# A tuned encoder trunk on one core: the first gated product kept in SBUF, the softmax's row maximum kept in PSUM, and one broadcast issued later

## The chip, the cores and the metric

The kernel runs on one core of a Trainium2 chip. The metric is the device time of one execution in microseconds, and the number compared is the median of several executions. Everything is float32 in memory; matrix products run in fp32r, each as three products of a high and a low part (hi x hi, hi x lo, lo x hi), so that nearly every operand has to be split into two tiles first.

## The reference

One encoder layer is applied to a prompt of 1024 tokens and to a sample of 256 tokens, both of width 1024. Cut to what matters here:

```python
y_a = deltanet_branch(...) @ w_up_a
y_b = spatial_gating_branch(...) @ w_up_b
merged = sigmoid(gate_a) * y_a + sigmoid(gate_b) * y_b
x = x + merged @ w_out
...
s = einsum('blhd,bmhd->bhlm', q, k) * XA_HEAD_DIM ** -0.5   # 4 heads, 256 memory tokens
p = softmax(s, axis=-1)
x = x + einsum('bhlm,bmhd->blhd', p, v).reshape(...) @ w_o
h = rmsnorm(x, norm_ffn_w)
gu = h @ ffn_w_gate_up
x = x + (silu(gu[..., :D_FF]) * gu[..., D_FF:]) @ ffn_w_down
```

A final RMS norm follows.

## The kernel before

**Layout.** Activations lie with channels on partitions, as tiles of 128 channels by tokens. `BLOCKS` cuts the 1280 tokens into two prompt blocks of 512 (b = 0, 1) and the sample's 256 (b = 2). A product of one output tile with one block is a chain of 128x512 or 128x256 matmuls into one PSUM bank. Two pools of four banks each (`pm`, `pq`) serve the whole program.

**What sets the order.** TensorE's instructions run in the order in which the Python code issues them. Main work is a generator; side work (norms, attention, loads) is a second set of generators that is let in when a planned clock, advanced by the cost of each issued matmul, passes the side's due time. Constants such as `LAGS2` are such due times, in planned nanoseconds. The other engines and the queues that issue transfers each work in one order of their own, which a scheduler derives from that code; an instruction that waits holds up all that stand behind it on its engine or queue. SyncE (SP) issues nearly all loads, ScalarE (ACT) some stores.

**Splitting.** `split` makes the high part on ScalarE (L125) and the low part on VectorE (DVE) or GpSimd (POOL) (L126); the low part is a subtraction of two SBUF tensors.

**The two ways up.** Both gates were computed earlier and stored in DRAM as `gtd`. `up_b` computes the spatial-gating branch's 8 x 3 products (24 jobs, tile m and block b). For each it loads the gate with `gate_load` into one of four `stage` slots, multiplies in place (L1132), and stores the result to DRAM (`tbd`, L1133, on ACT's queue). `up_a`, next, does the 24 products of the other branch: `merge_load` fetches its own gate (`ga`, L1200) and the stored result (`gb`, L1201); L1326 multiplies, and L1328 (prompt, into `mt`) or L1330 (sample) adds the two. While `up_b` runs, the side `load_ya` fetches `yod` and `sgd` (L1152), multiplies them (L1157) and splits them into the operands of `up_a`. `mt` has two tiles of the pool `hp`, under the tags hi0 and lo0; the memory's split tokens had these tags until `up_b` begins. Then comes the output projection (`Seven`), which needs `mt` split and combined.

**Attention.** For each of four heads and each 128 tokens, `scores` makes a 128x256 score tile in a bank. VectorE takes the negated row maximum (L1527) into a small SBUF tile `st`, multiplies it with the norm's factor `rstd`, also in SBUF (L1528); ScalarE exponentiates in the bank (L1530); VectorE takes the reciprocal (L1531) and scales into `e` (L1532), which frees the bank.

**Norms.** `Norm.rest` makes the mean on TensorE, the root on VectorE (L225 to L229, result `nst`), waits `lag2` of planned time, then issues the broadcast of the root over 128 partitions as matmuls of `nst` with the identity; VectorE then scales each tile (L285). The third norm, ahead of the feed-forward part, runs for each block as a side; `LAGS2` holds its `lag2` for the three blocks. `ff_first` is the first feed-forward step: its products with the sample come last in it.

Of the kernel before, what the change touches and what calls it, by code (L numbers as in the profile page):

```python
# [8 lines left out]
F32 = mybir.dt.float32  # L9
# [3 lines left out]
ALU = mybir.AluOpType  # L13
AX = mybir.AxisListType
# [3 lines left out]
P = 128  # L18
D = 1024
KT = D // P  # L20
NP, NS = 1024, 256
NTOK = NP + NS
NCH = NTOK // P
NMEM = 256
# [30 lines left out]
class Trunk:  # L55
# [54 lines left out]
    def mm3(self, ps, pairs, start=True, stop=True, more=False):  # L110

        last = len(pairs) - 1
        for i, (wh, wl, xh, xl) in enumerate(pairs):
            self.mm(ps, wh, xh, start and i == 0, False, more)
            self.mm(ps, wh, xl, False, False, more)
            self.mm(ps, wl, xh, False, stop and i == last, more)
            yield 0

    def tr(self, out, x, ident):
        self.clock += 64  # L120
        self.nc.tensor.transpose(out, x, ident)  # L121


    def split(self, hi, lo, src, eng=None):
        self.last_hi = self.nc.scalar.activation(hi, src, AF.Copy).ins  # L125
        (eng or self.nc.vector).tensor_tensor(out=lo, in0=src, in1=f32(hi), op=ALU.subtract)  # L126
# [37 lines left out]
def trunk_kernel(ctx: ExitStack, tc: tile.TileContext, a):  # L164
    nc = tc.nc
    V, S, G, T, SY = nc.vector, nc.scalar, nc.gpsimd, nc.tensor, nc.sync
# [3 lines left out]
    def pool(name, bufs=1, **kw):  # L170
        if kw.get("space") != DRAM:
            kw["reuse_waits"] = "tile"
        return tc.tile_pool(name=name, bufs=bufs, **kw)
# [3 lines left out]
    hp = ctx.enter_context(pool("h"))  # L177
    pm = ctx.enter_context(pool("pm", 4, space=PSUM))
    pq = ctx.enter_context(pool("pq", 4, space=PSUM))
    dp = ctx.enter_context(pool("dram", space=DRAM))  # L180
# [5 lines left out]
    n = 0  # L186
# [31 lines left out]
    def bank(p=pq, tag="b"):  # L218
        return p.tile([P, 512], F32, tag=tag, name="bank")
# [190 lines left out]
    yod = dp.tile([HEADS, P, NTOK], F32, name="yod")  # L410
    sgd = dp.tile([HEADS, P, NTOK], F32, name="sgd")
    gtd = dp.tile([16, P, NTOK], F32, name="gtd")
    tbd = dp.tile([KT, P, NTOK], F32, name="tbd")
    grd = dp.tile([2, 40, P], F32, name="grd")
    sqd = dp.tile([3, HEADS, P, NS], F32, name="sqd")

# [15 lines left out]
    ab = sp.tile([P, NCH, 16], F32, name="ab")  # L432
# [620 lines left out]
    def staging(n):  # L1053
        staged.append(0)
        return stage[:, len(staged) % 4, :n]
# [50 lines left out]
    def half_wk(w, i, k):  # L1106
        return wk(w, 4 * i + k)

    jobs = [(m, b) for m in range(KT) for b in range(3)]
    gates = []  # L1110

    def gate_load():
        if len(gates) < len(jobs):
            m, b = jobs[len(gates)]
            t0, n = BLOCKS[b]
            tb = staging(n)
            SY.dma_start(tb, gtd[8 + m, :, t0 : t0 + n])
            gates.append(tb)

    def up_b():  # L1120
        gate_load()
        for j, (m, b) in enumerate(jobs):
            if b == 0 and m % 2 == 0:
                w = K.take()
            gate_load()
            t0, n = BLOCKS[b]
            hi, lo = yb_h[b]
            ps = bank(pm)[:, :n]
            yield from mm3(ps, [(*half_wk(w, m % 2, k), hi[:, k, :], lo[:, k, :]) for k in range(4)])
            if m % 2 == 0 and b == 1:  # L1130
                K.ahead()
            V.scalar_tensor_tensor(out=gates[j], in0=gates[j], scalar=1.0, in1=ps, op0=ALU.add, op1=ALU.mult)  # L1132
            S.dma_start(tbd[m, :, t0 : t0 + n], gates[j])  # L1133

    y_h = []
    ues = ExitStack()
# [35 lines left out]
    def rest():  # L1172
        for m in range(1, KT):
            yield from mem_k(m)
        for h in range(HEADS):
            yield from mem_v(h)
        yield from up_b()
# [11 lines left out]

    up = K.up  # L1190
    merged = []
    mt = [hp.tile([P, KT, 512], F32, tag=tag, name="mt") for tag in ("hi0", "lo0")]
    smp_h = tuple(hp.tile([P, KT, NS], F32R, tag=tag, name=tag) for tag in ("hi2", "lo2"))

    def merge_load():
        if len(merged) < len(jobs):
            m, b = jobs[len(merged)]
            t0, n = BLOCKS[b]
            ta, tb = (up.tile([P, 512], F32, tag=f"g{x}", name=f"g{x}", bufs=4)[:, :n] for x in "ab")
            SY.dma_start(ta, gtd[m, :, t0 : t0 + n])  # L1200
            SY.dma_start(tb, tbd[m, :, t0 : t0 + n])  # L1201
            merged.append((ta, tb))

    class Seven:
# [306 lines left out]
    def attend(h, qh, ql, kh, kl, vh, vl, o_h):  # L1511
        es = {}

        def scores(b, c):
            g = 0 if b < 2 else 1
            t0 = BLOCKS[b][0]
            ts = slice(t0 + c * P, t0 + (c + 1) * P)
            ps = bank()[:, :NMEM]
            pairs = []
            for j in range(2):  # L1520
                ms = slice(j * 512 + g * NMEM, j * 512 + (g + 1) * NMEM)
                pairs.append((qh[:, j, ts], ql[:, j, ts], kh[:, ms], kl[:, ms]))
            for _ in mm3(ps, pairs):
                pass
            st = tp.tile([P, 4], F32, tag="st", name="st", bufs=8)
            r = rstd[:, t0 // P + c : t0 // P + c + 1]
            V.tensor_reduce(out=st[:, 3:4], in_=ps, axis=AX.X, op=ALU.max, negate=True)  # L1527
            V.tensor_tensor(out=st[:, 0:1], in0=st[:, 3:4], in1=r, op=ALU.mult)  # L1528
            e = tp.tile([P, NMEM], F32, tag="e", name="e", bufs=6)
            S.activation(ps, ps, AF.Exp, scale=r, bias=st[:, 0:1], accum_out=st[:, 1:2])  # L1530
            V.reciprocal(st[:, 2:3], st[:, 1:2])  # L1531
            V.tensor_scalar(out=e, in0=ps, scalar1=st[:, 2:3], scalar2=None, op0=ALU.mult)  # L1532
            es[b, c] = e

        def some(todo):
            if todo:
                b, c = todo.pop(0)
                scores(b, c)
                scores(b, c + 1)
                return A1  # L1540
            return 0

        todo = [(b, c) for b, (_, n) in enumerate(BLOCKS) for c in range(0, n // P, 2)]
        yield some(todo)
        yield some(todo)
        for b, (t0, n) in enumerate(BLOCKS):
            g = 0 if b < 2 else 1
            yield some(todo) + A2
            ppt = [bank(), bank()]
            pth, ptl = (tp.tile([P, 2, 512], F32R, tag=f"pt{i}", name=f"pt{i}") for i in range(2))  # L1550
            for j in range(2):
                for c in range(n // P):
                    tr(ppt[j][:, c * P : (c + 1) * P], es[b, c][:, j * P : (j + 1) * P], ident)
                split(pth[:, j, :n], ptl[:, j, :n], ppt[j][:, :n])
            yield some(todo) + A3
            for j in range(2):
                po = bank()[:, :n]
                pairs = []
                for mt in range(2):
                    vs = slice((2 * g + mt) * 256 + j * P, (2 * g + mt) * 256 + (j + 1) * P)  # L1560
                    pairs.append((vh[:, vs], vl[:, vs], pth[:, mt, :n], ptl[:, mt, :n]))
                for _ in mm3(po, pairs):
                    pass
                if o_h is None:
                    oo = tp.tile([P, 512], F32, tag="oo", name="oo", bufs=2)[:, :n]
                    S.activation(oo, po, AF.Copy)
                    S.dma_start(od[2 * h + j, :, t0 : t0 + n], oo)
                else:
                    hi, lo = o_h[b]
                    split(hi[:, 2 * h + j, :], lo[:, 2 * h + j, :], po)  # L1570
                yield A4
# [50 lines left out]
    op = OutProj(o_h, h3)  # L1622
# [638 lines left out]
MIX = 6500  # L2261
A1, A2, A3, A4 = 1200, 800, 2000, 600
DEC, CONV = 1200, 600
FIRST_W, PACES, LAGS2 = 9000, (600, 1300, 600), (2800, 9500, 7000)
LAGX = (26000, 17000, 9000)
LAG0, LAGF, LAGF2, PACEF = 7500, (8000, 6000, 1500), (9000, 9000, 2800), 1000

# [80 lines left out]
```

## Time and profile before

| | |
|---|---|
| median of 3 runs | 2226.89 us (2223.06 to 2227.9) |
| profiled execution, whole | 2224.42 us |
| its span in the trace | 2222.6 us |
| PE (matmul) busy | 2179.2 us, 98% of the span |
| PEld (weight load) busy | 1906.1 us, 86% |
| DVE, ACT, POOL busy | 1391.3, 866.9, 555.3 us |
| mean granted TensorE clock | 0.997 |

Times in the profile are microseconds from the span's start. A row of the timeline gives start, length, engine, line, operation, output and inputs, shape, and in brackets how long the engine had sat idle and what released it; "x2" merges two instructions. Lengths of successive matmuls overlap, since they are pipelined, so what a product costs TensorE is read from start to start.

### The profile page before, as it was taken

Reading aid. Unit: us, or ns where it says so; the run is one execution under the profiler, and the core shown is the slowest. Engines: PE = TensorE matmul, PEld = TensorE weight load, DVE = VectorE, ACT = ScalarE, POOL = GpSimd, SP = SyncE. Lnnn points to the kernel's source line nnn. Section 1 sums busy time; section 2 is a strip of 40 time slices with the busy share of each in tenths; the row PEclk is TensorE's granted clock in tenths of the full one; section 3 lists DMA queues with packets and bytes.
Section 4 is the critical chain, followed back from the end, with each engine's and each line's share of the span. In section 5 each row is a group of like instructions: output and inputs, shape, how many; then the busy total and the mean of one; then the engine's idle time right before and its main releaser. Section 6 shows DMA issues by size and latency. Waiting matters only on the chain.

```text
span 2222.6 us, 32341 instructions
## 1 busy us (share of the span) xinstructions
PE 2179.2 (98%) x12416; PEld 1906.1 (86%) x12416; DVE 1391.3 (63%) x2657; ACT 866.9 (39%) x1625; POOL 555.3 (25%) x358
## 2 busy tenths in 40 slices
PE   6999999999999999999999999999999999999998
PEld 5988889898988899888888888888888888888888
DVE  7767777786974864687654546734443444378575
ACT  5434153443525443124544423422322232343453
POOL 3010000000000000034421332466666666200031
PEclk9999999999999999999999999999999999999999
DMA  5222332223234455971421441222222222493631
GB/s 181 82 82 74 100 77 89 75 72 97 74 112 127 154 148 167 332 236 39 166 86 57 158 152 57 95 86 82 87 81 76 78 86 90 141 347 127 204 109 58
DMA packets 192821, 263.52 MB, mean 119 GB/s; under 512 B 72394, under 2 KB 102682, under 8 KB 192666
## 3 DMA queue, kind: packets, MB, share of 16 engines
q1 hardware_dynamic: 172826, 232.34, 31.8%
q10 hardware_dynamic: 19840, 29.11, 3.6%
q8 instruction: 97, 1.59, 0.3%
q14 instruction: 58, 0.48, 0.1%
HBM read 183.24 MB, written 78.16 MB: 118 GB/s over the span
## 4 chain that ended last, share of the span: by engine, by line
PE 82%; DVE 6%; issue 5%; DMA 4%; ACT 1%; POOL 1%; SPq 0%; POOLq 0%; ACTq 0%; DVEq 0%
PE bank L108 81%; PE bank L121 1%; DMA tbd<-stage 1%; DMA braw<-gq 1%; DVE wlo L1232 0%; DVE xf L126 0%; DMA stage<-gtd 0%; DVE lo L126 0%; DVE x L1441 0%; DMA t<-sgd 0%; DMA gb<-tbd 0%; DMA r<-in_w_out 0%; DVE nacc L250 0%; DVE wlo L126 0%; DVE nt L285 0%
## 5 line engine op out<-in xcount | busy, mean ns | idle before, releaser
L108 PE MATMUL bank<-hi,whi 128*128 128x512 f32 (+1 forms) x1976 | 701.9, 355 | 0.0
L108 PE MATMUL bank<-hi,wlo 128*128 128x512 f32 (+1 forms) x1976 | 687.0, 348 | 0.0
L108 PE MATMUL bank<-lo,whi 128*128 128x512 f32 (+1 forms) x1976 | 686.8, 348 | 0.0
L108 PEld LDWEIGHTS bank<-hi,wlo 128*128 128x128 f32 x1976 | 373.6, 189 | 48.8
L108 PEld LDWEIGHTS bank<-hi,whi 128*128 128x128 f32 x1976 | 374.4, 189 | 43.8 <-issue 0.2
L108 PEld LDWEIGHTS bank<-lo,whi 128*128 128x128 f32 x1976 | 374.6, 190 | 43.4 <-issue 0.2
L125 ACT ACTIVATE whi<-raw 128x1024 fp32r<-128x1024 f32 (+1 forms) x136 | 137.0, 1010 | 258.3 <-PE bank L108 219.2
L126 POOL TENSOR_TENSOR wlo<-raw,whi 128x1024 fp32r<-128x1024 f32 x65 | 157.2, 2420 | 307.4 <-ACT whi L125 307.4
L108 PE MATMUL bank<-bhl,whi 128*128 128x512 f32 x408 | 125.9, 390 | 0.1
L126 DVE TENSOR_TENSOR wlo<-raw,whi 128x1024 fp32r<-128x1024 f32 (+1 forms) x71 | 81.7, 1151 | 66.0 <-ACT whi L125 65.6
L126 POOL TENSOR_TENSOR wlo<-x,whi 128x1024 fp32r<-128x1024 f32 x40 | 97.4, 2435 | 47.6 <-ACT whi L125 47.6
L2013 DVE TENSOR_TENSOR x<-x,bank 128x512 f32<-128x512 f32 x21 | 14.5, 688 | 125.5 <-ACT x L1808 125.5
L108 PEld LDWEIGHTS bank<-bhl,whi 128*128 128x128 f32 x408 | 76.5, 188 | 16.5 <-ACT whi L125 0.5
L615 DVE SCALAR_TENSOR_TENSOR acc<-craw,sm,acc 128x510 f32<-128x510 f32 (+1 forms) x96 | 72.9, 759 | 25.9 <-ACT acc L613 24.2
L1821 DVE SCALAR_TENSOR_TENSOR t<-t,x 128x512 f32<-128x512 f32 x42 | 64.2, 1530 | 28.4 <-ACT t L1820 28.4
L108 PE MATMUL bank<-bhl,wlo 128*128 128x512 f32 x204 | 79.7, 391 | 0.7 <-DVE wlo L126 0.5
L125 ACT ACTIVATE whi<-x 128x1024 fp32r<-128x1024 f32 (+1 forms) x48 | 49.0, 1025 | 79.9 <-PE bank L108 73.7
L250 DVE TENSOR_TENSOR nacc<-nacc,nsq 128x512 f32<-128x512 f32 (+1 forms) x68 | 58.0, 852 | 34.0 <-ACT nsq L249 32.8
L1830 DVE SCALAR_TENSOR_TENSOR t<-bank,t 128x512 f32<-128x512 f32 (+1 forms) x44 | 24.5, 558 | 82.5 <-PE bank L108 82.5
L108 PE MATMUL bank<-bhl,ahl 128*128 128x512 f32 x312 | 75.0, 395 | 0.0
L883 POOL COPY UT<-U 64x512 f32<-64x512 f32 x20 | 14.9, 752 | 238.8 <-PE bank L108 235.8
L982 ACT ACTIVATE gs<-bank 128x512 f32<-128x512 f32 (+1 forms) x60 | 31.1, 518 | 108.3 <-PE bank L108 102.9
(373 smaller groups left out, 4578.5 us busy)
## 6 DMA issues: line engine op xcount, KB each, us to landing
raw<-in_w_gu SPq DMA_DIRECT2D x44, 512.0 KB, 3.5
braw<-gq SPq DMA_DIRECT2D x14, 1024.0 KB, 7.2
raw<-in_w_g SPq DMA_DIRECT2D x20, 512.0 KB, 3.3
gq<-t SPq DMA_DIRECT2D x33, 256.0 KB, 2.0
gtd<-gs ACTq DMA_DIRECT2D x32, 256.0 KB, 2.2
w<-in_w_dn SPq DMA_DIRECT2D x8, 1024.0 KB, 12.4
raw<-in_w_qkv SPq DMA_DIRECT2D x12, 512.0 KB, 3.6
gq<-r SPq DMA_DIRECT2D x22, 256.0 KB, 2.1
```

The costliest lines, as they stand in the source:

```text
L108: self.nc.tensor.matmul(out, l, r, start=start, stop=stop, skip_group_check=more)
L121: self.nc.tensor.transpose(out, x, ident)
L125: self.last_hi = self.nc.scalar.activation(hi, src, AF.Copy).ins
L126: (eng or self.nc.vector).tensor_tensor(out=lo, in0=src, in1=f32(hi), op=ALU.subtract)
L250: (eng or V).tensor_tensor(out=self.acc, in0=self.acc, in1=sq, op=ALU.add)
L615: V.scalar_tensor_tensor(out=dst, in0=src, scalar=wj, in1=dst, op0=ALU.mult, op1=ALU.add)
L883: G.tensor_copy(Um[q, hs, :], U[d][q, hs, :])
L982: S.activation(t, ps, AF.Tanh, scale=0.5)
L1821: V.scalar_tensor_tensor(out=t, in0=t, scalar=1.0, in1=src, op0=ALU.add, op1=ALU.mult)
L1830: V.scalar_tensor_tensor(out=out, in0=u, scalar=sign, in1=t, op0=ALU.mult, op1=ALU.mult)
L2013: V.tensor_tensor(out=c22, in0=c22, in1=pe, op=ALU.add)
```

## The change

Three independent edits.

1. The gated result of `up_b` for the two prompt blocks is written straight into `mt` (allocated earlier for that), not to `stage` and DRAM, and `up_a` adds to it in place. Only the sample's result still goes through `tbd`. `up_b` also loads its gates two jobs ahead where it loaded one ahead.
2. The negated row maximum goes into column 256 of the bank that holds the scores, not into `st`.
3. `LAGS2` of the sample is 9500 where it was 7000, so the broadcast of its root is issued later.

```diff
     def up_b():
-        gate_load()
+        mt.extend(hp.tile([P, KT, 512], F32, tag=tag, name="mt") for tag in ("hi0", "lo0"))
+        for _ in range(2):
+            gate_load()
...
-            V.scalar_tensor_tensor(out=gates[j], in0=gates[j], scalar=1.0, in1=ps, op0=ALU.add, op1=ALU.mult)
-            S.dma_start(tbd[m, :, t0 : t0 + n], gates[j])
+            out = mt[b][:, m, :] if b < 2 else gates[j]
+            V.scalar_tensor_tensor(out=out, in0=gates[j], scalar=1.0, in1=ps, op0=ALU.add, op1=ALU.mult)
+            if b == 2:
+                S.dma_start(tbd[m], out)
...
-            ta, tb = (up.tile([P, 512], F32, tag=f"g{x}", name=f"g{x}", bufs=4)[:, :n] for x in "ab")
+            ta = up.tile([P, 512], F32, tag="ga", name="ga", bufs=4)[:, :n]
             SY.dma_start(ta, gtd[m, :, t0 : t0 + n])
-            SY.dma_start(tb, tbd[m, :, t0 : t0 + n])
+            if b < 2:
+                tb = mt[b][:, m, :]
+            else:
+                tb = up.tile([P, NS], F32, tag="gb", name="gb", bufs=3)
+                SY.dma_start(tb, tbd[m])
...
-            ps = bank()[:, :NMEM]
+            pb = bank()
+            ps, mx = pb[:, :NMEM], pb[:, NMEM : NMEM + 1]
...
-            V.tensor_reduce(out=st[:, 3:4], in_=ps, axis=AX.X, op=ALU.max, negate=True)
-            V.tensor_tensor(out=st[:, 0:1], in0=st[:, 3:4], in1=r, op=ALU.mult)
+            V.tensor_reduce(out=mx, in_=ps, axis=AX.X, op=ALU.max, negate=True)
+            V.tensor_tensor(out=st[:, 0:1], in0=mx, in1=r, op=ALU.mult)
...
-FIRST_W, PACES, LAGS2 = 9000, (600, 1300, 600), (2800, 9500, 7000)
+FIRST_W, PACES, LAGS2 = 9000, (600, 1300, 600), (2800, 9500, 9500)
```

Lines behind the edits move by up to ten: L1152 becomes L1158, L1200 becomes L1205, L1201 becomes L1210, L1218 becomes L1227.

On TensorE the only instruction that moves is the broadcast of edit 3. Before it stood one step ahead of the end of the product with `b21`, the second half of the first block's operand (hi_12890 here):

```order
L108 MATMUL bank<-hi_12890,wlo 128x512
L108 MATMUL bank<-cst,nst 128x128 x2
L108 MATMUL bank<-hi_12890,whi 128x512
L108 MATMUL bank<-lo_12891,whi 128x512
L108 MATMUL bank<-hi_12890,wlo 128x512
L108 MATMUL bank<-hi_12892,whi 128x512
```

Now that product (hi_12842 here) is finished first, and nine matmuls with the second block's `b22` (hi_12844) stand ahead of the broadcast too:

```order
L108 MATMUL bank<-hi_12842,wlo 128x512
L108 MATMUL bank<-hi_12844,whi 128x512
L108 MATMUL bank<-lo_12845,whi 128x512
L108 MATMUL bank<-hi_12844,wlo 128x512
L108 MATMUL bank<-hi_12844,whi 128x512
L108 MATMUL bank<-lo_12845,whi 128x512
L108 MATMUL bank<-hi_12844,wlo 128x512
L108 MATMUL bank<-hi_12844,whi 128x512
L108 MATMUL bank<-lo_12845,whi 128x512
L108 MATMUL bank<-hi_12844,wlo 128x512
L108 MATMUL bank<-cst,nst 128x128 x2
L108 MATMUL bank<-hi_12844,whi 128x512
```

The broadcast is issued twelve matmuls of 128x512 later. What VectorE does with it moves too. Before, from the end of the root (`nst`) on, where x_12580 is the sample's tile and x_12578 and x_12579 are those of the prompt blocks:

```order
L229 SCALAR_TENSOR_TENSOR nst<-bank,nst 128x2
L126 TENSOR_TENSOR lo_12893<-x_12578,hi_12892 128x1024
L285 SCALAR_TENSOR_TENSOR x_12580<-x_12580,sm,bank 128x256 x2
L1830 SCALAR_TENSOR_TENSOR t<-bank,t 128x512
L126 TENSOR_TENSOR lo_12895<-x_12580,hi_12894 128x256
L285 SCALAR_TENSOR_TENSOR x_12580<-x_12580,sm,bank 128x256 x4
```

Now, from the same place, the sample's tile being x_12532:

```order
L229 SCALAR_TENSOR_TENSOR nst<-bank,nst 128x2
L1840 SCALAR_TENSOR_TENSOR t<-bank,t 128x512
L126 TENSOR_TENSOR lo_12845<-x_12530,hi_12844 128x1024
L285 SCALAR_TENSOR_TENSOR x_12532<-x_12532,sm,bank 128x256 x4
L126 TENSOR_TENSOR lo_12847<-x_12532,hi_12846 128x256
L285 SCALAR_TENSOR_TENSOR x_12532<-x_12532,sm,bank 128x256
L126 TENSOR_TENSOR lo_12847<-x_12532,hi_12846 128x256
L285 SCALAR_TENSOR_TENSOR x_12532<-x_12532,sm,bank 128x256
L126 TENSOR_TENSOR lo_12845<-x_12530,hi_12844 128x1024
L126 TENSOR_TENSOR lo_12847<-x_12532,hi_12846 128x256
L1831 SCALAR_TENSOR_TENSOR t<-t,bank 128x512
L285 SCALAR_TENSOR_TENSOR x_12532<-x_12532,sm,bank 128x256 x2
```

Other work of the prompt blocks goes ahead of the sample's scalings, and the last two of the eight come behind a 128x512 step of the gate. On SP's queue, in `up_b`, the fetches of `load_ya` stood in pairs behind each other:

```order
L1152 DMA t_8951<-yod 128x2x512
L1152 DMA t_8952<-sgd 128x2x512
L1152 DMA t_8987<-yod 128x2x512
L1152 DMA t_8988<-sgd 128x2x512
L1117 DMA stage<-gtd 128x512 x2
L1117 DMA stage<-gtd 128x256
```

Now each pair stands behind one more load of a gate:

```order
L1158 DMA t_8950<-yod 128x2x512
L1158 DMA t_8951<-sgd 128x2x512
L1117 DMA stage<-gtd 128x512
L1158 DMA t_8985<-yod 128x2x512
L1158 DMA t_8986<-sgd 128x2x512
L1117 DMA stage<-gtd 128x512
L1117 DMA stage<-gtd 128x256
```

The second pair now waits behind a gate's load, which needs a free `stage` slot. Of `up_a`'s loads in this queue the sixteen `gb` loads of the prompt are gone.

More of the change, by code (lines that the diff above doesn't have):

```diff
@@ L412, in trunk_kernel @@
     gtd = dp.tile([16, P, NTOK], F32, name="gtd")
-    tbd = dp.tile([KT, P, NTOK], F32, name="tbd")
+    tbd = dp.tile([KT, P, NS], F32, name="tbd")
     grd = dp.tile([2, 40, P], F32, name="grd")
@@ L1118, in gate_load @@
             gates.append(tb)
+    mt = []
     def up_b():
-        gate_load()
+        mt.extend(hp.tile([P, KT, 512], F32, tag=tag, name="mt") for tag in ("hi0", "lo0"))
+        for _ in range(2):
+            gate_load()
         for j, (m, b) in enumerate(jobs):
@@ L1191, in trunk_kernel @@
     merged = []
-    mt = [hp.tile([P, KT, 512], F32, tag=tag, name="mt") for tag in ("hi0", "lo0")]
     smp_h = tuple(hp.tile([P, KT, NS], F32R, tag=tag, name=tag) for tag in ("hi2", "lo2"))
```

## The prediction

> **What bounds the kernel now.** First the page's busy times, then what TensorE waited for, then the stretches around the three edits.
>
> ```profile
> PE 2179.2 (98%) x12416; PEld 1906.1 (86%) x12416; DVE 1391.3 (63%) x2657; ACT 866.9 (39%) x1625; POOL 555.3 (25%) x358
> PE bank L108 <- DVE nst L229: 7.2, 5, 2.3
> PE bank L108 <- DVE e L1532: 2.0, 2, 1.8
> PE bank L108 <- DVE stage L1132: 1.7, 4, 0.8
> PE bank L108 <- DVE ga L1326: 1.0, 2, 0.5
> ```
>
> TensorE is the bound: of the 2222.6 us span 2222.6 - 2179.2 = 43.4 us are idle, so no edit that leaves its products alone can win more than its own small part of that. The four waiting rows (total, times, longest) name the places: a root (nst), the softmax (e), and the two ways up (stage, ga). The edits touch one wait of the first row and the other three rows. The change is thus worth single microseconds; 0.2% of this kernel, about what a measurement can tell from no change, is 4.45 us.
>
> **Edit 1, the ways up.** The windows give length, then PE, PEld and DVE busy, and near the end clock, DMA share and GB/s:
>
> ```profile
> 880.00:900.00 20.00, 20.00 (x107) 17.24 (x106) 12.51 (x14) 4.24 (x4) 0.00 (x0) 1.00 0.98 321
> 900.00:920.00 20.00, 18.75 (x97) 15.22 (x96) 10.62 (x15) 3.38 (x4) 0.00 (x0) 1.00 0.85 288
> 920.00:940.00 20.00, 19.57 (x97) 16.18 (x96) 11.44 (x16) 3.49 (x4) 2.40 (x1) 1.00 1.04 381
> 940.00:960.00 20.00, 19.04 (x100) 15.84 (x99) 18.32 (x26) 4.53 (x7) 2.40 (x1) 1.00 0.81 270
> SPq L1117 <- DMA tbd<-stage: 35.1, 10, 6.7
> DVE stage L1132 <- DMA stage<-gtd: 9.3, 5, 3.3
> DVE t L1157 <- DMA t<-sgd: 5.1, 5, 1.7
> tbd<-stage ACTq DMA_DIRECT2D x16, 256.0 KB, 4.1
> gb<-tbd SPq DMA_DIRECT2D x11, 256.0 KB, 4.4
> ```
>
> The DMA engines are full from 880 to 940. SP stood 35.1 us on gate loads, because a stage slot is free only once its store to tbd has landed; VectorE then stood 9.3 us on late gates, and TensorE ran out of banks. PE idle from 900 to 960 is 1.25 + 0.43 + 0.96 = 2.64 us. From start to start it is more:
>
> ```profile
> 904.10 0.28 PE L108 MATMUL bank<-yb,wlo 128*128 128x256 f32 x1
> 905.16 0.70 PE L108 MATMUL bank<-yb,whi 128*128 128x512 f32 x2 [0.78 <-DVE stage L1132]
> 946.74 0.39 PE L108 MATMUL bank<-yhi,wlo 128*128 128x512 f32 x1
> 947.61 0.39 PE L108 MATMUL bank<-yhi,whi 128*128 128x256 f32 x1 [0.48 <-DVE ga L1326]
> 987.33 1.06 ACT L125 ACTIVATE xf<-mt 128x1024 fp32r<-128x1024 f32 x1 [4.83 <-PE bank L108]
> 988.42 2.41 DVE L126 TENSOR_TENSOR xf<-mt,xf 128x1024 fp32r<-128x1024 f32 x1 [5.67 <-ACT xf L125]
> ```
>
> A 256-wide matmul otherwise starts 0.12 us after the last, a 512-wide one 0.23 us, so the first gap costs 1.06 - 0.12 = 0.94 where 0.78 is listed, the second 0.87 - 0.23 = 0.64 where 0.48 is listed: 0.16 more each. For the six waits that is 2.64 + 6 x 0.16 = 3.6 us. The change takes away 16 stores and 16 loads of 256 KB, 8.4 MB of what the full DMA engines move here; a slot is then freed by L1132 itself, not by a store's landing, and the gates are fetched one job earlier. L1132 writes the same number of elements, and hi0 and lo0 are free, since the products that read the memory's tokens stand earlier on TensorE: that costs nothing. The sample's eight stores and loads stay. I take all 3.6. Bounds: 1.7, the stage row alone (late t<-sgd may still hold up VectorE), and 4.0, if the slow start after each gap (about 0.07) goes too. Does the gain survive? The last two rows say yes: when up_a ends, ACT and VectorE have idled 4.83 and 5.67 us and are released by TensorE's own last product, so the work behind shifts with it.
>
> **Edit 2, the row maximum.** The first five rows are of the first head's start, the others of the last head's start:
>
> ```profile
> 1112.13 2.41 POOL L126 TENSOR_TENSOR wlo<-raw,whi 128x1024 fp32r<-128x1024 f32 x1
> 1112.20 2.36 DVE L1528 TENSOR_TENSOR st<-st,rstd 128x1 f32<-128x1 f32 x1
> 1115.41 0.39 PE L108 MATMUL bank<-hi,wlo 128*128 128x512 f32 x1
> 1116.02 1.68 PE L108 MATMUL bank<-kv,q 128*128 128x256 f32 x12 [0.22 <-DVE e L1532]
> 1116.92 0.16 DVE L1528 TENSOR_TENSOR st<-st,rstd 128x1 f32<-128x1 f32 x1
> ...
> 1118.00 0.48 DVE L1532 TENSOR_SCALAR e<-bank,st 128x256 f32<-128x256 f32 x1
> ...
> 1246.89 1.25 DVE L1528 TENSOR_TENSOR st<-st,rstd 128x1 f32<-128x1 f32 x1
> 1248.51 0.85 DVE L1528 TENSOR_TENSOR st<-st,rstd 128x1 f32<-128x1 f32 x1
> ...
> 1247.84 0.39 PE L108 MATMUL bank<-hi,wlo 128*128 128x512 f32 x1
> 1250.01 2.00 PE L108 MATMUL bank<-kv,q 128*128 128x256 f32 x12 [1.78 <-DVE e L1532]
> ```
>
> A product of two columns of one element takes 0.16 us, but 2.36 when GpSimd runs a subtraction: it ends with that (1114.56 against 1114.54). Both of L1528's inputs lie in SBUF. The root's L228 shows what one input in PSUM does (length min/median/max in ns):
>
> ```profile
> L228 DVE TENSOR_TENSOR bank<-bank,nst x30: 160/170/171, 11.5 to 2214.7; 128x4 f32<-128x4 f32 x21, 128x2 f32<-128x2 f32 x9
> L228 DVE TENSOR_TENSOR cw<-cw x30: 155/166/169, 219.3 to 868.6; 128x8 f32<-128x8 f32 x30
> L228 DVE TENSOR_TENSOR sums<-sums x9: 148/155/2355, 50.2 to 126.2; 128x4 f32<-128x4 f32 x6, 128x2 f32<-128x2 f32 x3
> ```
>
> With two SBUF inputs 2355 ns occurs, in PSUM never over 171. So L1528 should take 0.16 to 0.17 everywhere. First place: 0.61 - 0.23 = 0.38 us from start to start, gone, since e comes 2.2 us earlier. Last head: 2.17 - 0.23 = 1.94 us lost, and the twelve matmuls then take 0.32 longer than at 1116.02, behind the second bank. An undisturbed chain puts e 1118.00 - 1116.92 = 1.08 us behind L1528, so e runs from 1247.97 to 1248.45, TensorE starts at 1248.51 where it could at 1248.07, and 0.44 stays: 1.94 - 0.44 + 0.32 = 1.8. Together 2.2 us. Bounds: 0.4 (the first place alone, if GpSimd then holds up a neighbour) and 2.7 (no rest). In PSUM the operand costs 170 - 166 = 4 ns or 170 - 155 = 15 ns; the maximum's write into PSUM is not in the trace, and the nearest rows, these, allow 0.02 us a tile, on VectorE's own time.
>
> [...]
>
> **Edit 3, the broadcast.**
>
> ```profile
> 1387.05 0.39 PE L108 MATMUL bank<-hi,wlo 128*128 128x512 f32 x1
> 1388.48 0.15 DVE L229 SCALAR_TENSOR_TENSOR nst<-bank,nst 128x2 f32<-128x2 f32 x1
> 1388.78 0.68 PE L108 MATMUL bank<-cst,nst 128*128 128x128 f32 x4 [1.34 <-DVE nst L229]
> ...
> 1394.86 1.88 DVE L126 TENSOR_TENSOR lo<-x,hi 128x1024 fp32r<-128x1024 f32 x2
> 1400.89 0.28 PE L108 MATMUL bank<-hi,whi 128*128 128x256 f32 x1
> 1416.97 2.31 DVE L126 TENSOR_TENSOR wlo<-raw,whi 128x512 fp32r<-128x512 f32 x1
> 1420.47 0.39 PE L108 MATMUL bank<-whi 128*128 128x512 f32 x1
> ```
>
> TensorE loses 1.73 - 0.23 = 1.50 us here. Twelve matmuls later the broadcast stands at 1387.28 + 12 x 0.227 = 1390.0, the root is there at 1388.63, so the wait goes. What is late next hangs on VectorE, which is without a pause from 1388.5 to 1419.3. The sample's splits end at 1396.74, 4.15 us ahead of their products; now they begin 1.2 us later and the last two fall behind other work, about 1399.0, while TensorE comes to them at 1399.4 and to the last ones 1.4 later: enough, just. The fused weight (wlo from raw) is tighter: both halves now come behind all of VectorE's queue, at about 1419.3 to 1420.3, and TensorE wants the first at 1418.97. I charge 0.7 of the possible 0.3 to 1.3 and keep 0.8 us; bounds 0 and 1.5.
>
> **Sum:** 3.6 + 2.2 + 0.8 = 6.6 us, bounds 2.1 and 8.2. The profiled execution would go from 2224.42 to 2217.8. That execution lies low among the four known times (2223.06 to 2227.9, mean 2225.6), so I set the sum against the mean: 2219.0 us.
>
> **Rivals.**
> - *The ways up give their time back.* Behind up_a the output projection's splits on VectorE and GpSimd run long, and TensorE, earlier, waits there. Against it stands the idle time at 987. It would cost edit 1: 3.0 us gained, 2222.6. Chance 0.17.
> - *Edit 2 does not do it.* GpSimd still blocks the step, or the neighbouring subtraction on the last head takes the time. Against: the L228 rows. 4.4 us gained, 2221.2. Chance 0.11.
> - *Slower: SP's queue starves load_ya.* Each pair's t<-sgd now stands behind one more gate load, which waits for a slot; L1157 waits for t<-sgd, and L1132, which frees slots, stands behind it on VectorE. Price: six fetches, each late by up to one 512-wide job, 12 x 0.227 = 2.7 us, make 16.4 us. VectorE has 40 - 23.1 = 16.9 us free from 880 to 920, of which 9.3 + 5.1 are waits already, so 13.9 would be left over; four banks hide about four jobs, 9.2, and 4.7 reaches TensorE. With edits 2 and 3 that is 1.7 us slower, 2227.3. It decides from the point where the t<-sgd row passes 5.1 + 2.5 + 9.2, about 17 us. Against: fewer bytes make all loads land sooner. Chance 0.10.
>
> **How the numbers follow.** The forecast has 0.62. Range: from the fastest run less 8.2, 2214.9, to the slowest less 2.1, 2225.8, rounded out to 2214.5 to 2226; it holds the first two rivals too. Faster by over 0.2% is the forecast and half of the second rival, 0.68; the slower rival lies mostly within 0.2%, but its price is open upwards: slower 0.08; the rest, 0.24, is within.
>
> **What would show it.** Right: no PE waits on stage or ga between 880 and 960, the SPq row on tbd gone, DMA share clearly under 0.9; L1528's successor at most 0.2 us, PE waits on e under 0.6 in all; the broadcast without a wait, and at most one short PE wait on wlo some 30 us behind it. Wrong: new PE waits between 990 and 1060 (first rival), a long product on st (second), a t<-sgd row over 10 us (third), or a wait of over 1.5 us behind the broadcast.

## The result, and the profile after

The changed kernel takes 2211.96 us in the median of 6 runs (2211.58 to 2214.07), the kernel before 2226.12 in 6 runs beside them (2223.06 to 2227.9): ratio 0.9946, 95% interval 0.9936 to 0.9956 (a ratio here is an estimate from the single runs; the quotient of these two medians would be 0.9936). A second measurement, with 23 runs of the kernel before, gave 2223.64 and 2212.28: ratio 0.9951, interval 0.9938 to 0.9963, 11.4 us. The direction was forecast, the size was not: 6.6 us were expected and the median lies below the range. (Two runs of the experiments, 2394 and 2780 us at a mean granted clock of 0.85 and 0.73, are left out of every spread below.)

First the busy times of the changed kernel, then two rows of what TensorE waited for, then the same three windows as before.

```profile
PE 2174.5 (98%) x12416; PEld 1905.6 (86%) x12416; DVE 1383.3 (63%) x2657; ACT 866.9 (39%) x1625; POOL 557.5 (25%) x358
PE bank L108 <- DVE nst L229: 3.8, 3, 2.3
PE bank L108 <- DVE e L1542: 0.3, 1, 0.3
900.00:920.00 20.00, 20.00 (x107) 17.25 (x106) 11.82 (x17) 3.38 (x4) 0.00 (x0) 1.00 0.88 299
920.00:940.00 20.00, 20.00 (x106) 17.25 (x105) 16.92 (x21) 3.91 (x5) 4.79 (x2) 1.00 0.73 257
940.00:960.00 20.00, 20.00 (x106) 17.26 (x105) 17.73 (x29) 5.39 (x7) 0.00 (x0) 1.00 0.52 155
```

The rows for stage and ga are gone, and e is down from 2.0 to 0.3. The nst row falls from 7.2 to 3.8, but only 1.34 us of that is the sample's broadcast; the rest lies elsewhere, and a second trace of the changed kernel has 5.8. TensorE is never idle on the ways up. The DMA share, 0.85, 1.04 and 0.81 before, is 0.88, 0.73 and 0.52: it falls mostly in `up_a`. The queues there, from 860 to 960 (SP's wait, two of VectorE's), and the softmax step that had taken up to 2.36 us (length min/median/max in ns):

```profile
SPq L1117 <- DMA tbd<-stage: 19.3, 5, 7.7
DVE t L1163 <- DMA t<-sgd: 4.0, 3, 2.0
DVE mt L1137 <- DMA stage<-gtd: 1.9, 1, 1.9
L1538 DVE TENSOR_TENSOR st<-bank,rstd x40: 144/158/159, 1104.3 to 1256.6; 128x1 f32<-128x1 f32 x40
```

**Where the time went.** Both programs issue the same matmuls in the same order but for the one broadcast of edit 3. Laying the two traces over each other, matmul by matmul, and taking the shift of the start at both ends of a stretch (times of the first trace of before) gives what each stretch won (-) or lost (+), in us:

| trace | start to 898 | ways up 898-958 | output projection 1010-1060 | first head 1110-1125 | last head 1235-1260 | broadcast 1380-1400 |
|---|---|---|---|---|---|---|
| all three edits | -1.72 | -4.79 | -1.37 | -0.47 | -1.83 | -1.60 |
| all three, again | -1.31 | -4.79 | -1.37 | -0.47 | -1.81 | -1.57 |
| edit 1 alone | -2.28 | -4.79 | -1.37 | +0.12 | 0.00 | 0.00 |
| edit 2 alone | -1.03 | +1.41 | +0.01 | -0.47 | -1.81 | 0.00 |
| edit 3 alone | -1.45 | +1.77 | +0.01 | -0.22 | +0.01 | -1.57 |
| before, again | -2.44 | -0.05 | +0.01 | -0.24 | +1.42 | +0.01 |
| two gates ahead only | -0.84 | -0.27 | -0.02 | -0.35 | +1.47 | 0.00 |

The first column belongs to no edit: all of its shift arises before 860, where the programs do the same, and their traces still lie up to 2.4 us apart. In the other columns every trace with an edit agrees to 0.03 us, while traces without it scatter: the kernel before loses 4.7 to 6.6 us on the ways up and 1.8 to 3.3 in the last head. In its two traces the changed kernel is not only faster there, it is the same both times.

The gain in the output projection was not forecast. Rows of the timeline, of before, around the second pair of splits and the two waits that follow, then of the changed kernel at the same place:

```profile
1000.97 2.40 POOL L1232 TENSOR_TENSOR al<-r,ah 128x1024 fp32r<-128x1024 f32 x1 [1.16 <-ACT ah L1231]
1001.05 3.40 DVE L1232 TENSOR_TENSOR wlo<-r,whi 128x1024 fp32r<-128x1024 f32 x1
1018.24 0.50 PE L108 MATMUL bank<-xf,ah 128*128 128x512 f32 x1 [0.18 <-DVE xf L126]
1056.46 0.47 PE L108 MATMUL bank<-xf,whi 128*128 128x512 f32 x1 [0.51 <-DVE x L1441]
```

```profile
981.91 1.89 DVE L126 TENSOR_TENSOR xf<-mt,xf 128x1024 fp32r<-128x1024 f32 x1 [6.14 <-ACT xf L125]
994.02 1.21 DVE L1241 TENSOR_TENSOR wlo<-r,whi 128x1024 fp32r<-128x1024 f32 x1
994.47 3.02 POOL L1241 TENSOR_TENSOR al<-r,ah 128x1024 fp32r<-128x1024 f32 x1 [1.70 <-ACT ah L1240]
```

Before, GpSimd's subtraction began 0.08 us ahead of VectorE's, which then took 3.40 us; now VectorE's begins 0.45 ahead, takes 1.21, and GpSimd pays (3.02 for 2.40). VectorE is early because its xf split, 2.41 us before, took 1.89: GpSimd's row of subtractions began 0.48 us earlier against TensorE, since VectorE, without late gates, had no backlog at the end of up_a. The same split of the same shape thus took VectorE 3.40 us where GpSimd had begun first, and 1.21 us where VectorE had.

### The profile page after: what moved, and what is told of

Same layout as the page of the kernel before. It is cut to its first block, busy times and chain, and to the rows that moved or that the text cites. A ratio compares the mean times of both kernels' runs of the same rounds, so it can differ in the third digit from the quotient of the medians.

```text
span 2211.0 us, 32271 instructions
## 1 busy us (share of the span) xinstructions
PE 2174.5 (98%) x12416; PEld 1905.6 (86%) x12416; DVE 1383.3 (63%) x2657; ACT 866.9 (39%) x1625; POOL 557.5 (25%) x358
## 4 chain that ended last, share of the span: by engine, by line
PE 88%; issue 5%; DVE 3%; DMA 1%; ACT 1%; POOL 1%; SPq 0%; POOLq 0%; ACTq 0%; DVEq 0%
PE bank L108 87%; PE bank L121 1%; DMA mraw<-md 0%; DMA raw<-in_w_sv 0%; DVE nt L285 0%; ACT hi L125 0%; DVE lo L126 0%; POOL nacc L250 0%; DVE wlo L126 0%; DMA raw<-in_w_u 0%; DVE nacc L250 0%; POOL x L281 0%; ACT whi L125 0%; DVE gt L427 0%; DVE sums L228 0%
```

## The experiments

**Each edit alone.** The diffs are those of the change, one part each.

> Edit 1 alone, whole. Theory A (the two profiled executions are typical): 4.8 us on the two ways up plus 1.3 us in the output projection, 6.1 us faster, ratio 0.9973; its runs lie as far apart as those of before (about 5 us). Theory B (the stalls that edit 1 removes hang on how the transfers fall and are mostly larger than in the profiled execution of before): 8 to 10 us faster, ratio 0.9955 to 0.9964, and its runs lie within about 2.5 us, as those of the changed kernel. Theory C (the prediction's size): 3.6 us, ratio 0.9984, nothing in the output projection.

> Edit 2 alone. Theories A and B: 2.2 to 2.4 us faster, ratio 0.9990, L1528's successor never over 0.2 us, one wait on e of about 0.3 us left in the last head. A rival (GpSimd's subtractions slow another step of the chain): under 1 us. By theory B its runs still lie about 5 us apart, because the ways up are those of before.

> Edit 3 alone: 1.5 to 2.0 us faster, ratio 0.9992, no wait on nst at the sample's broadcast and none on the fused weight's wlo (the prediction charged 0.7 us for that one and had 0.8). If the charge comes true here, 0.8 us. By theory B its runs lie about 5 us apart, as those of before.

> The changed kernel again, beside the three single edits. Theory A: the ratio is about 0.9955 (10 us) and the single edits add up to it (6.1 + 2.4 + 1.6). Theory B: 0.9937 to 0.9950 (11 to 14 us), of which edit 1 has 8 to 10. If the edits help one another, the whole is over 1.5 us more than the sum of the three.

Measured beside 23 runs of before (2223.64): edit 1 2217.09, ratio 0.9971 (0.9960 to 0.9982); edit 2 2221.91, 0.9990 (0.9981 to 0.9999); edit 3 2222.94, 0.9998 (0.9989 to 1.0007); all three 2212.28, 0.9951. The medians do not settle whether the edits add up. Their gains, 6.55, 1.73 and 0.70 us, sum to 9.0 where the whole has 11.4; the 2.4 us between are more than the 1.5 that I had named for edits that help one another, but each interval reaches 2 to 3 us to either side. Edit 3 alone, for which I had expected 1.5 to 2.0, cannot be told from no change by its runs. The traces do settle it: in the table, the stretches of the whole are those of the single edits, to 0.03 us. For edit 1 theory A has the size (6.55 us), and theory C, the prediction's size, is out. Theory B has the scatter, as far as so few runs show it: runs with the old ways up spread over 6.0, 5.3 and 6.4 us (before, 23 runs; edits 2 and 3, 10 each), with the new ones over 2.6 and 2.7 (7 and 5 runs); two later versions with the new ones spread over 3.3 and 3.8 (4 and 5 runs). That the old ways up change from one execution to the next shows in TensorE's waits from 880 to 960, with edit 2 alone and then with edit 3 alone (1.7 and 1.0 us in the first trace of before):

```profile
PE bank L108 <- DVE stage L1132: 2.4, 3, 1.2
PE bank L108 <- DVE ga L1326: 1.6, 3, 1.0
```

```profile
PE bank L108 <- DVE stage L1132: 2.3, 4, 1.1
PE bank L108 <- DVE ga L1326: 2.1, 2, 1.1
```

**Which half of edit 1.** In the changed kernel, one gate ahead; in the kernel before, two ahead; in the changed kernel, the prompt's results stored as well.

```diff
-        for _ in range(2):
-            gate_load()
+        gate_load()
```

> The changed kernel with the gates loaded one job ahead again (only the SBUF half of edit 1, with edits 2 and 3). If the SBUF half does it alone (a slot is freed by the product, the transfers are halved): no PE wait on stage or mt between 880 and 960 of over 0.5 us in all, within 1 us of the changed kernel, ratio to before about 0.995. If the second gate ahead is what keeps VectorE from waiting: 2 us or more slower than the changed kernel, ratio about 0.9960 to 0.9965, with waits on L1137 in the ways up.

> The kernel before with only the second gate ahead; the result still goes through DRAM. By the reading that a slot comes free only when its store has landed, asking earlier gains nothing: SP stands longer on tbd (over 35 us) and holds up load_ya; no faster than before, 0 to 3 us slower, ratio 1.000 to 1.0015. If depth alone were the remedy: 4 us faster, ratio 0.998.

```diff
-            if b == 2:
-                S.dma_start(tbd[m], out)
+            S.dma_start(tbd[m, :, t0 : t0 + n], out)
```

> The changed kernel, which also stores all of the prompt's gated results to DRAM as before (nobody reads them; 16 stores of 256 KB are back, the slots still come free at once). If the slots held by stores were the stall: as the changed kernel, ratio 0.995, the tbd waits of SP unchanged. If the full DMA engines were the stall: DMA share near 0.95 again from 900 to 940, gates and sgd landing later, 1 to 3 us slower than the changed kernel, and runs up to 5 us apart.

One gate ahead: 2215.03 (4 runs from 2211.96), ratio 0.9951 (0.9934 to 0.9968), and its trace wins 4.79 and 1.37 as the whole does, with no wait of TensorE on the ways up. Four runs are too few for the time to decide (the quotient of the medians is 0.9960, which I had given to the other answer); the trace decides: the SBUF half does the work. Two ahead alone: 2221.52, ratio 0.9987 (0.9977 to 0.9996), while its trace wins only 0.27 on the ways up; SP's wait on tbd grew to 38.0 us, as I had expected. I had expected no gain, so depth helps the median a little where the result goes through DRAM, and it isn't needed where it doesn't. With the stores kept: 2216.87, 0.9961 (0.9946 to 0.9976), its 4 runs 5.0 us apart, and the DMA share is back at 0.97 and 0.93 from 900 to 940. Up to 926, in up_b and the first jobs of up_a, its trace wins 2.48 us, as the whole does; from there to 958 it is 3.6 us behind the whole. The first two rows are VectorE, the next three TensorE, the last is the window from 940 (clock in the third column from the right):

```profile
932.10 0.43 DVE L126 TENSOR_TENSOR lo<-ga,hi 128x256 fp32r<-128x256 f32 x1 [4.19 <-DMA tbd<-stage]
934.98 3.10 DVE L126 TENSOR_TENSOR xf<-mt,xf 128x1024 fp32r<-128x1024 f32 x1 [1.13 <-ACT xf L125]
938.74 0.39 PE L108 MATMUL bank<-yhi,whi 128*128 128x256 f32 x1 [1.77 <-DVE ga L1334]
940.35 0.63 PE L108 MATMUL bank<-yhi,whi 128*128 128x512 f32 x1
940.78 0.63 PE L108 MATMUL bank<-ylo,whi 128*128 128x512 f32 x1
940.00:944.00 4.00, 4.00 (x14) 3.24 (x13) 4.00 (x6) 1.21 (x2) 0.00 (x0) 0.57 0.67 210
```

So both suspects count, at different places. With free slots `up_b` runs through even with the stores (from 880 to 1060 the 1.77 in `up_a` is TensorE's only listed wait). In `up_a` VectorE stands 4.19 us until the sample's last store has landed (first row), and TensorE waits for it later; in the changed kernel the same split, at 926.47, had idled only 0.55 us and was released by ScalarE. Whether their bytes delay it or their places in ACT's queue, this run does not separate. And a stall can cost more than its length: from 1.4 us behind the wait of 1.77 the clock is granted at half (0.57 in the window of 4 us), matmuls of 128x512 start 0.43 us apart instead of 0.23, and 1.5 us more are lost.

**The race in the output projection.** A step of VectorE more in up_a's 23rd job:

```diff
+            if j == 22:
+                V.tensor_scalar(out=ta[:, :400], in0=ta[:, :400], scalar1=1.0, scalar2=None, op0=ALU.mult)
```

> The changed kernel with one more step of VectorE, a product with 1.0 in place of 128x400 elements (about 0.48 us), in up_a's 23rd job. In the traces GpSimd's row of subtractions at the output projection began 0.48 us earlier against TensorE than in the kernel before, since VectorE's backlog was gone, and the two PE waits on xf and x there (1.27 us with what follows them) went. [...] If the gain there came from elsewhere: no wait there, 0 us.

2214.39, ratio 0.9952 (0.9938 to 0.9967), as the changed kernel; its trace shows more. The added step took 0.37 us, and against the changed kernel GpSimd began 0.30 us later relative to TensorE. I had put about 1.3 us of loss between 1010 and 1050 if the order in which the two engines begin decides. Nothing was lost there; 1.23 us were lost at 998, in one wait:

```profile
992.41 2.81 DVE L1241 TENSOR_TENSOR wlo<-r,whi 128x1024 fp32r<-128x1024 f32 x1
998.27 0.73 PE L108 MATMUL bank<-xf,ah 128*128 128x512 f32 x2 [0.95 <-DVE x L1460]
```

The wlo split is long again (2.81 for 1.21), and what is late is the eviction queued behind it (x). But the scheduler has also moved this split: it now stands ahead of five evictions that go before it in the changed kernel. So the run shows that a held split can cost TensorE over 1 us here (1.23), not that the 0.30 us alone did it. That the order of the two steps made the 1.37 us is read from the rows of before and after; it was not isolated.

**How far the broadcast may move.**

```diff
-... LAGS2 = ..., (2800, 9500, 9500)
+... LAGS2 = ..., (2800, 9500, 12000)
```

> The changed kernel with LAGS2 of the sample at 12000: the broadcast stands 12 more matmuls (2.7 us) later. In the changed kernel the sample's last split ends near 1389.0 and TensorE needs it at about 1391.6, so by the bounds of the prediction's edit 3 the cover is nearly used up: 0.1 to 1.5 us lost between 1385 and 1412, on the sample's hi or lo, or on the fused weight's wlo. If the cover is wider than I read it: 0 us, the same as the changed kernel.

2214.49 in one run, and its trace wins 1.57 at the broadcast, as with 9500. The scheduler has moved VectorE's steps along with the broadcast, so the cover that I read off the changed kernel was not the one that counts; with the order of this run 12 more matmuls cost nothing.

**The kernel before once more.**

> The kernel before, profiled once more. If its stalls on the ways up hang on how the transfers fall, TensorE's loss from 898 to 958 is not 4.8 us against the changed kernel again but lies somewhere between 4.5 and 6.6 (the two single edits that share this code showed 6.2 and 6.6), and the loss in the output projection (1.37) and at the broadcast (1.6) is the same to 0.1 us. If the stalls are fixed, 4.8 again.

2222.51 us in the one run. The loss on the ways up was 4.74, nearly that of the first trace, so this run alone does not speak for the scatter; the four traces with this code show 4.74, 4.79, 6.20 and 6.56. Output projection and broadcast were the same to 0.01 us. The new thing was the last head, 1.42 us worse than in the first trace. The wait is the same 1.78, but the clock behind it isn't, 0.57 where the first trace has 1.00 up to 1256 (timeline, then the window):

```profile
1247.27 2.66 PE L108 MATMUL bank<-kv,q 128*128 128x256 f32 x12 [1.78 <-DVE e L1532]
1248.00:1252.00 4.00, 3.97 (x16) 3.29 (x15) 3.51 (x13) 1.96 (x7) 0.94 (x1) 0.57 0.37 131
```

**Edit 2's remedy at another place**, on the changed kernel:

```diff
-        rsqrt(rs[:, cs], var[:, cs], s0[:, cs])
+        rsqrt(rs[:, cs], var[:, cs], bank()[:, : cs.stop - cs.start])
```

> The changed kernel, with edit 2's remedy at one more place: the scratch of the root in ln (the sums of the spatial gating branch) lies in a PSUM bank, not in SBUF. In every trace so far its product of two SBUF columns near 121 takes 2.35 us beside a GpSimd subtraction, the vg tiles come late, TensorE waits 1.3 us for them near 129, and 6 matmuls behind that run at half rate (0.66 us more). If the second SBUF input is what locks the product: it takes 0.17 us, vg is up to 2.2 us earlier, the wait goes: 1.3 to 2.0 us faster than the changed kernel, ratio to before about 0.994. If another step on VectorE is locked in its place (the first vg step of 512 elements, by GpSimd's next subtraction): the wait stays, 0 us.

2213.13, ratio 0.9953 (0.9939 to 0.9966): no gain, and the wait on vg stays (1.3 us). The timeline of the changed kernel (second run), then of this one:

```profile
121.93 2.42 POOL L126 TENSOR_TENSOR wlo<-raw,whi 128x1024 fp32r<-128x1024 f32 x1 [42.10 <-ACT whi L125]
122.01 2.35 DVE L228 TENSOR_TENSOR sums<-sums 128x4 f32<-128x4 f32 x1
```

```profile
122.53 2.42 POOL L126 TENSOR_TENSOR wlo<-raw,whi 128x1024 fp32r<-128x1024 f32 x1 [42.87 <-ACT whi L125]
122.62 0.16 DVE L228 TENSOR_TENSOR bank<-bank,sums 128x4 f32<-128x4 f32 x1
122.73 2.32 DVE L490 SCALAR_TENSOR_TENSOR wk<-wk 128x80 f32<-128x80 f32 x1
```

The product is free (0.16 for 2.35), and the next step with two SBUF inputs is held in its place (2.32 for 0.24). This shows what edit 2 does, and why it worked in the softmax: there, the steps behind the product read a bank or a single SBUF tensor, and of the 40 of each none was held (at most 433, 166 and 487 ns at L1537, L1541 and L1542 of the changed kernel). A split ahead of it in the last head has two SBUF inputs, and is held in the changed kernel as it was before (2.23 us for 128x512; the split of that size at 1413.50 of before took 0.68):

```profile
1236.39 2.23 DVE L126 TENSOR_TENSOR lo<-oraw,hi 128x512 fp32r<-128x512 f32 x1
```

**GpSimd out of the way**, on the changed kernel, for the weights of the last block of that branch:

```diff
     for b in (2, 0, 1):
+        K.lo_vector = b == 1
```

> The changed kernel with the low parts of the spatial gating branch's weights from the last block on (GpSimd's subtractions near 122, 127 and 146) made on VectorE. In ln_psum the lock only moved from the root's product to the next step with two SBUF inputs; here GpSimd has no subtraction at that time. If the lock is the cause of TensorE's wait on vg near 130: no step of VectorE over 1.3 us from 120 to 131, the wait of 1.3 us and the six half-rate matmuls behind it (0.66) go, less what VectorE's own two subtractions cost (1.2 us each, in place of two locks of 2.2): 1.3 to 2.0 us faster than the changed kernel, ratio to before about 0.9943. If the wait has another cause, or VectorE is then late for the weights: 0 us or slower.

2212.55, ratio 0.9950 (0.9937 to 0.9964), as the changed kernel. The edit moved the second and the third subtraction; the first stayed on GpSimd and held the root's product for 2.35 us as before, so my condition (no such step from 120 to 131) was not met. With the second on VectorE the vg steps ran unheld and the wait on vg went: 2.0 us were won, but 1.1 came back at once. The 0.9 us that its trace keeps are too small for five runs to show. What TensorE waited for, in the changed kernel (second run) and here:

```profile
PE bank L108 <- DVE vg L458: 1.3, 1, 1.3
```

```profile
PE bank L121 <- DVE gr L505: 1.2, 1, 1.2
```

In both expectations I took the six matmuls behind the vg wait for half-rate ones. The clock granted to the changed kernel from 130.3 to 132 is 1.00: they were paced by the vg tiles (in the first trace the weight loads stood 0.16 us for vg ahead of each of the last two pairs). No version was measurably better than the changed kernel.

## Why the prediction was wrong in size

- **The bound** held, as TensorE issues the same products, but listed idle time was not all there was to win. From 860 to 1440 (times of before), where the edits act, TensorE took 10.1 us less, of which 6.4 were listed as idle (7.8 before, 1.4 now) and 3.6 counted as busy: slow starts and short delays hide in it (the two matmuls behind the wait at 905.16 took 0.70 us, two at 1000.51 took 0.62).
- **Edit 1, 3.6 us with 4.0 at most:** mis-sized, 4.79 against this very trace. I added the six idle times that the trace lists. It measures them from modelled ends that overlap by 0.16 us, so delays below that are not listed at all, and the slow start behind each gap went into the bound alone. The quoted windows had the answer in their counts: 97 + 97 + 100 = 294 matmuls from 900 to 960, where now there are 107 + 106 + 106 = 319; 25 x 60 / 319 = 4.7 us. And one execution was taken for typical: four traces of this code average 5.6.
- **"The work behind shifts with it":** the step that failed most clearly. The rows at 987 showed ACT and VectorE released by TensorE; GpSimd hung on VectorE's backlog (through ScalarE's high parts) and came 0.48 us earlier. 1.37 us were won where nothing was expected and a rival feared a loss.
- **The SPq row on tbd gone:** no, 19.3 us are left, from the sample's eight stores. It held up nobody on TensorE's path, and the t<-sgd row, 5.1 us before, is 4.0 and 6.1 us in the two traces of the changed kernel, far from the 10 that I had named; the rival of the starved queue did not come.
- **Edit 2, 2.2 us:** the mechanism and the size of this trace were right (0.47 + 1.83 = 2.30; 0.27 of a wait on e left, 0.44 forecast). The PSUM operand costs nothing that shows: the product takes 158 ns in the median with it, 160 before. What was missing is the half clock behind the 1.78 us stall in some executions: over the five traces without the edit the last head costs 2.39 us and the first 0.33, together 2.7. The last section says when the traces have it.
- **Edit 3, 0.8 us:** the loss of 1.50 was right (1.57 to 1.60 won), the charge of 0.7 for the late fused weight wrong. It was priced from a split that GpSimd held up, 2.31 us for 512 columns. Now GpSimd pays: it comes at 1407.14 into a row of VectorE's steps that run without a pause, and ends only at 1411.40 (4.26 us, where the 65 of its kind take 2.45 in the mean). Both of VectorE's are done by 1409.1, and TensorE takes the first low part at 1409.14, not when it takes the high one (1408.69, the moment I had used):

```profile
1404.95 2.35 DVE L126 TENSOR_TENSOR t4l<-x,t4h 128x1024 fp32r<-128x1024 f32 x2
1407.14 4.26 POOL L126 TENSOR_TENSOR wlo<-raw,whi 128x1024 fp32r<-128x1024 f32 x1 [9.59 <-ACT whi L125]
1407.22 0.68 DVE L1831 SCALAR_TENSOR_TENSOR t<-t,x 128x512 f32<-128x512 f32 x1
1407.83 1.28 DVE L126 TENSOR_TENSOR wlo<-raw,whi 128x512 fp32r<-128x512 f32 x2
```

- **The base:** 2225.6 came from four runs. The 54 runs of before beside the experiments have medians of 2223.6 to 2224.1.

The corrected sum, 5.6 + 1.4 + 2.7 + 1.6 = 11.3 us, is made of averages of four and five traces; it meets the 11.4 measured against 23 runs of before, but the edits alone measured less (1.73 for 2.7 and 0.70 for 1.6, both within their intervals). Of the error of 7.0 us, 4.8 is the sum (6.6 for 11.4) and the rest the base and the draw of runs. Why the first six runs of before lay 2.0 to 2.5 us higher than the medians of the later ones stays open.

## What to carry to other kernels

Count a bound engine's instructions in equal windows before and after a stall region: lost instructions times the pitch come close to the true loss (4.7 for 4.79 here), and listed idle times fell short of it (2.64). Where a subtraction of GpSimd and a split of VectorE run at the same time, as here at the output projection, which of them began first went with which took longer (VectorE's 3.40 or 1.21 us, GpSimd's 2.40 or 3.02), and it was the other way round in the trace where GpSimd's row began 0.48 us earlier; so look for gains and losses far behind an edit, and take the price of a held step only for as long as the order stands. A stall that hangs on transfers differed here from one execution to the next (4.74 to 6.56 us over four traces); price it from several traces, or at least put its whole spread into the range.

## What the runs showed of the hardware

A stall of 1.77 to 1.79 us on TensorE was followed, past the first 30 us, in three of six cases by a stretch at half the granted clock (0.57 in a window of 4 us in two of them, 0.69 and 0.89 in the two windows that the third reaches over) that began 0.9 to 1.4 us after the restart and cost 1.4 to 1.5 us; of the 19 stalls of 1.3 us (near 130, 715 and 1388 in the traces of all kernels) two were.

Why it comes only in some executions has a reading in the traces. Each records the clock as a list of stretches. Within one trace, up to its last 20 us, every half-clock stretch is 3.41 us long or twice that, and they begin a whole number of 3.41 us apart (with the stores kept: at 49.243, 131.163 and 940.122 us, 24 and 237 times 3.413). So each of these traces can be laid on a grid of 3.41 us, which lies differently in each: half-clock stretches begin at 27.56 us in the first trace of before and at 50.18 in that of the changed kernel, 0.25 and 2.40 us behind a whole number of 3.413. Where the six long stalls lie in it, counted in intervals from the start of the one in which the stall begins:

| trace | stall, us | from | to | half clock in the next interval |
|---|---|---|---|---|
| before, last head | 1.78 | 0.62 | 1.14 | no |
| edit 1 alone, last head | 1.79 | 0.63 | 1.15 | no |
| edit 3 alone, last head | 1.77 | 0.50 | 1.02 | no |
| before again, last head | 1.78 | 0.22 | 0.75 | yes |
| two gates ahead only, last head | 1.78 | 0.19 | 0.71 | yes |
| stores kept, ways up | 1.77 | 0.08 | 0.59 | yes |

The three that fit whole into one interval brought the half clock, the three that reach over its end did not. If the grid lies at random, an estimate from these lengths is that a stall of 1.78 us fits whole in (3.41 - 1.78) / 3.41 = 48% of executions. This is read from six cases and was not tested. It does not sort the stalls of 1.3 us: of the nine that fit whole one brought the half clock, of the ten others one.
